# Hybrid decoder step on one core: the final norm's factors from a product with a matrix of ones, and the decode attention's output one step earlier in the output projection

## The chip, the core and the metric

The kernel runs on one core of a Trainium2 chip. A core has five engines that run side by side and wait for one another by semaphores: TensorE (PE; its weight loads are shown apart as PEld), VectorE (DVE), ScalarE (ACT), GpSimd (POOL) and SyncE (SP, which here only starts transfers). Each engine takes its instructions strictly in the order in which they were written into its queue. PE writes to the accumulator memory PSUM, which has eight banks; all else lies in the on-chip memory SBUF or in DRAM.

The metric is the device time of one execution in microseconds (us). The kernel before took a median of 1489.31 us in three runs (1488.1 to 1490.61).

## The reference

One layer of a decoder trunk over 1024 prompt tokens and 8 samples of one token each (T = 1032 columns in all). What the change touches:

```python
def rmsnorm(x, g):
    xf = x.astype(jnp.float32)
    y = xf * lax.rsqrt(jnp.mean(xf * xf, axis=-1, keepdims=True) + EPS)
    return (y * g.astype(jnp.float32)).astype(x.dtype)
...
oa_d = diff_attention(qa_d, k_all, v_all, pos_d, kpos_d, rel_bias, lam)
...
xd = xd + merge_groups(oa_d, o_rd, gr_d, subln_a[l], lam_init).astype(xd.dtype) @ w_out[l]
...
xp = xp + sq_relu_mlp(rmsnorm(xp, norm_mlp[l]), w_up[l], w_down[l])
...
y_prompt = rmsnorm(xp, norm_final)
y_sample = rmsnorm(xd, norm_final)
```

The output projection takes the attention's result for all 1032 tokens; the 8 samples' part needs each sample's attention over its cached values, normalized per head. The last step is a norm over the 1024 features of each token.

## The kernel before, in words

Everything is held transposed: features on the 128 partitions (eight groups `ft`), tokens along the row. A product in fp32 precision is made of three products of rounded halves (`UH`, `UL` for the operand, `wh`, `wl` for the weights), so each tile of the output projection has 8 x 3 = 24 matmuls. A scheduler places the instructions of a stage in the queues by its own estimate of the times; where `pin[0]` is set, PE keeps the order of the program. `issue_after` keeps an instruction from being placed ahead of another.

*The output projection* (`proj_residual`, tiles `pr_o`) runs over 8 feature groups and 3 column parts of 344 tokens, first parts 0 and 1 of all groups, then part 2, which holds the samples. The tile (ft, c) is added to the residual on DVE (line 1447), squared on ACT, and its squares are summed on GpSimd. Beside it runs a generator, `decode_values`, which makes the samples' attention output. After each tile listed in the argument `when` it takes one step: eight steps that gather a row of cached values and add its weighted sum to `dacc` on DVE; one that adds the new token's value; one (`dop`, `oda`) that sums `dacc` over groups of partitions on PE, copies the result, and normalizes it on DVE and GpSimd; and one (`dtr`) that transposes it on PE and splits it into `UH` and `UL`. Before the change, the last two steps were taken at the two places in `stage`: after tile (7, 1), the first half of part 2 for groups 0 and 1 is computed, then `dop`'s step is taken; then the first half for groups 2 to 4, then `dtr`'s. The second half of part 2 reads what `dtr` gave.

*The final norm* is made within the MLP's down projection (tiles `dn`), in its last group of steps, in program order. The steps n = 0 to 15 are the products for column half c = 0 (n = 0 to 7), then c = 1. The squares of the result are summed over the feature groups into `ssumf` (128 partitions by 1032 tokens). For each of the four quarters of tokens (c, half), 258 columns each, `finish_columns` and `finish_rows` run after the steps listed in two tables. `finish_columns` takes three pieces of 86 columns as stationary operands against a column of ones, so that the sums over partitions come out as 86 x 3; ACT takes the square root, DVE the reciprocal of that small tile (`factor_columns`). `finish_rows` spreads the factors back over 128 partitions by three products with the identity (`factor_rows`), and DVE multiplies the result's tiles by what stands in PSUM. For the second half the last tile's squares, `tails`, come as a second product and not through `ssumf`. The last quarter (1, 1) is finished after the last product of the program.

Of the kernel before, what the change touches and what calls it, by code (L numbers as in the profile page):

```python
# [10 lines left out]
F32 = mybir.dt.float32  # L11
# [8 lines left out]
P = 128  # L20
D = 1024
# [27 lines left out]
def decoder_step(ctx: ExitStack, tc: tile.TileContext, i: dict, o: dict):  # L49
    nc = tc.nc  # L50
# [1465 lines left out]
    with pool("x2") as XP:  # L1516
        x2 = [XP.tile([P, T], F32, tag=f"x2_{ft}", name=f"x2_{ft}") for ft in range(8)]
        g_mq = XP.tile([P, 8], F32, tag="g_mq", name="g_mq")
        nc.sync.dma_start(g_mq, i["g_mq"])
        with pool("c") as A:  # L1520
            def decode_values():
                def dt(name):
                    return PB.tile([P, 512], F32, tag="av", name=name, bufs=1)

                acc = A.tile([P, T], F32, tag="dacc", name="dacc")
                for k in range(8):
                    raw = A.tile([P, 1024], F32, tag="draw", name=f"cv_{k}", bufs=4)
                    gather(raw, i["cache_v"], idx, k)
                    with tc.issue_after(seen["DVE"]):
                        for x in range(8):  # L1530
                            c = slice(x * P, x * P + P)
                            w = at[:, x % 4, 2 * k + x // 4 : 2 * k + x // 4 + 1]
                            if k == 0:
                                nc.vector.tensor_scalar(acc[:, c], raw[:, c], w, None, ALU.mult)
                            else:
                                nc.vector.scalar_tensor_tensor(acc[:, c], raw[:, c], w, acc[:, c], ALU.mult, ALU.add)
# [8 lines left out]
                nc.vector.tensor_add(acc[:, :512], acc[:, :512], pd[:, :512])  # L1545
                yield

                with tc.issue_after(seen["PE"]):
                    op = dt("dop")
                    mm(op[:8, :], selgt, acc[:, 0:512], True, True)  # L1550
                    mm(op[32:40, :], selgt, acc[:, 512:1024], True, True)
                    od2 = A.tile([P, 1024], F32, tag="draw", name="oda", bufs=4)
                    oda, sqd = od2[:8, 0:512], od2[:8, 512:1024]
                    nc.scalar.copy(oda, op[32:40, :])
                    nc.vector.tensor_add(oda, oda, op[:8, :])
                    nc.vector.tensor_mul(sqd, oda, oda)
# [5 lines left out]
                    nc.vector.tensor_mul(odv, odv, r4.unsqueeze(2).to_broadcast([8, 4, P]))  # L1562
                yield
                with tc.issue_after(seen["PE"]):
                    tr = dt("dtr")
                    for h in range(4):
                        nc.tensor.transpose(tr[:, h * 8 : h * 8 + 8], oda[:, h * P : h * P + P], ident[:8, :8])
                    odT = tr[:, :32].rearrange("p (k c) -> p k c", k=4)
                    for h in range(4):
                        split_gain(odT[:, h, :], subln8, h, NT, T, gcol=0)  # L1570
                yield


            ssum = A.tile([P, T], F32, tag="ssum", name="ssum2")
            last = proj_residual(
                A, out_bank, U_OUT, OUT_KT, lambda ft: i["xT"][:, ft, :], lambda ft: x2[ft], ssum, "o", us_out, decode_values(),
                [(ft, c) for ft in range(4) for c in range(2)] + [(4, 1)],
                lambda x: [
                    G.tile([P, T], F32R, tag="rb2", name="wlo_3")[:, :1024] if (nm, x) == ("wl", 7)
                    else A.tile([P, 1024], F32R, tag=f"{nm}{x}", name=f"{nm}o_{x}") for nm in ("wh", "wl")  # L1580
                ],
                ahead=len(OUT_EARLY), early=early_out, stage=([(0, 2), (1, 2)], [(2, 2), (3, 2), (4, 2)]),
            )
# [392 lines left out]

    QP = QC // 3

    def factor_columns(bank, sums, last, x):
        col = bank[:QP, 300:303]  # L1980

        terms = [(y, j) for y in (sums, last) if y is not None for j in range(3)]
        for n, (y, j) in enumerate(terms):
            pinned(nc.tensor.matmul(
                col[:, j : j + 1], y[:, j * QP : j * QP + QP], ones[:, :1], start=n == 0, stop=n >= len(terms) - 3,
                skip_group_check=True))
        fc = KC.tile([QP, 3], F32, tag=f"fc{x % 2}", name=f"fc_{x}", bufs=2)
        nc.scalar.activation(fc, col, AF.Sqrt, scale=1.0 / D, bias=epsc[:QP])
        nc.vector.reciprocal(fc, fc)
        return fc  # L1990
# [7 lines left out]

    def norm_factor(x):
        fp = PD.tile([P, 512], F32, tag=("mk", "dt")[x % 2], name=f"rm_{x}", bufs=1)  # L2000
        FACTORS[x] = fp, factor_columns(fp, ssum[:, QCOLS[x]], None, x)

    def norm_rows(x):
        nc.scalar.copy(ssum[:, QCOLS[x]], factor_rows(*FACTORS[x]))
# [236 lines left out]
    with pool("acc", side="right") as AC, pool("rd", side="right") as RD, pool("w") as A, pool("w_ps", space=PSUM) as PS:  # L2241
# [19 lines left out]

        COLUMNS_AT, ROWS_AT, tails = {0: (0, 0), 3: (1, 0), 10: (0, 1), 15: (1, 1)}, {2: (0, 0), 5: (1, 0), 12: (0, 1), 15: (1, 1)}, {}
# [61 lines left out]
        ends = {}  # L2326

        def finish_columns(c, half):
            fp = PS.tile([P, 512], F32, tag=f"acc{turns[0] % 8}", name=f"fin_{c}_{half}", bufs=1)
            turns[0] += 1  # L2330
            ends[c, half] = fp, factor_columns(fp, ssf[:, QCOLS[2 * c + half]], tails[c] if half else None, 4 + 2 * c + half)
            for ft in range(8):
                y = C[((11, 21), (12, 22))[half][ft // 4]][:, ft % 4, c * QC : c * QC + QC]
                nc.scalar.activation(y, y, AF.Copy, scale=g_fin[:, ft : ft + 1])

        def finish_rows(c, half):
            cs = QCOLS[2 * c + half]
            rf = factor_rows(*ends[c, half])
            n = 2 if (c, half) == (1, 1) else 4
            for ft in range(0, 8, n):  # L2340
                y = C[((11, 21), (12, 22))[half][ft // 4]][:, ft % 4 : ft % 4 + n, c * QC : c * QC + QC]
                nc.vector.tensor_mul(y, y, rf.unsqueeze(1).to_broadcast([P, n, QC]))
                (nc.scalar if n == 2 and ft % 4 else nc.sync).dma_start(
                    o["yT"][ft * P : (ft + n) * P, cs].rearrange("(f p) c -> p f c", p=P), y)

        pin[0] = True
        for g in range(4):
# [26 lines left out]
            for new, qs, ps_ in parts:  # L2374
# [23 lines left out]
                for n, (q, p, c) in enumerate(steps):  # L2398
# [15 lines left out]
                    if g == 3:  # L2414
                        shared = C[0][:, p, cq]
                        for quad in {6: (21, 12), 7: (22,)}.get(q, ()):
                            nc.gpsimd.dma_start(C[quad][:, p, cq], shared, accum_op=ALU.add)
                        tail = None
                        if q in (2, 4, 5, 3):
                            tail = squares(INTO[q], p, c, (q, p) == (3, 3))  # L2420
                        if tail is not None:
                            tails[c] = tail
                        if end and n in COLUMNS_AT:
                            finish_columns(*COLUMNS_AT[n])
# [202 lines left out]
```

## Time and profile before

| | |
|---|---|
| Median of three runs | 1489.31 us (1488.1 to 1490.61) |
| The profiled execution | 1496.69 us, its span 1494.8 us |
| Busy share of PE, DVE, ACT, POOL | 98%, 73%, 45%, 21% |
| Output projection with decode output | about 455 to 537 us |
| Last products of the down projection | end at about 1484 us |
| From there to the end of the span | about 11 us |

A row of a timeline has the start in us, the duration in us, the engine, the line, the operation, what it writes and reads, the shape, the count, and in brackets the idle time ahead of it with what ended it. A piece of the chain has start, duration, engine, tile, line and count. A row of the windows has the stretch and its length, the busy time of PE, PEld, DVE, ACT and POOL with counts, the granted clock of TensorE, the share of the DMA engines, and GB/s. Matmuls overlap: a record is longer than the distance to the next. One fp32 matmul of the program shows as two records.

### The profile page before, as it was taken

How to read it: one execution, taken by the hardware profiler on the slowest of the kernel's cores; microseconds unless marked ns; L12 is line 12 of the kernel's file. 1: busy time of each engine (PE TensorE's matmuls, PEld its weight loads, DVE VectorE, ACT ScalarE, POOL GpSimd, SP SyncE). 2: the span in 40 equal slices, each digit the busy share in tenths (PEclk: the TensorE clock that was granted, in tenths of full speed). 3: DMA queues.
4: the chain of work that ended last, by engine and by line, in shares of the span. 5: the costliest groups of instructions: out<-in, count | busy, mean ns of one | idle time of the engine just before them, and what ended most of it. 6: DMA issues, size and time to landing. Idle time of an engine off the chain costs nothing.

```text
span 1494.8 us, 27880 instructions
## 1 busy us (share of the span) xinstructions
PE 1471.7 (98%) x10925; PEld 1401.8 (94%) x10925; DVE 1098.7 (73%) x2264; ACT 679.6 (45%) x1325; POOL 321.1 (21%) x346
## 2 busy tenths in 40 slices
PE   9999999998999999999999999999999999999997
PEld 7899779998779999989999999999999999999997
DVE  7666436887767636567886988888888879787865
ACT  7543435665552431248535643434334443343454
POOL 0035323123414311105022100000001311110380
PEclk9999999999999999999999999999999999999998
DMA  8255728213847157474582444344436774536273
GB/s 287 65 185 180 202 58 189 71 47 110 268 145 283 59 195 175 145 228 102 178 304 68 136 148 145 128 154 157 156 139 209 239 251 142 171 101 198 72 128 114
DMA packets 125238, 236.69 MB, mean 158 GB/s; under 512 B 13748, under 2 KB 76521, under 8 KB 124978
## 3 DMA queue, kind: packets, MB, share of 16 engines
q1 hardware_dynamic: 89064, 170.51, 36.0%
q0 software_dynamic: 24912, 44.80, 11.0%
q10 hardware_dynamic: 11130, 19.60, 3.5%
q8 instruction: 86, 1.41, 0.4%
q14 instruction: 46, 0.38, 0.1%
HBM read 170.25 MB, written 57.52 MB: 152 GB/s over the span
## 4 chain that ended last, share of the span: by engine, by line
PE 84%; DVE 8%; ACT 3%; issue 2%; DMA 2%; POOL 0%; ACTq 0%; another core or an unknown queue 0%; SPq 0%; DVEq 0%; POOLq 0%
PE dn L2309 19%; PE Z L2143 9%; PE qkp L75 7%; PE mq L75 6%; PE Y L2143 6%; PE X L2143 6%; PE pr_o L75 6%; PE pr_m L75 4%; PE grp L75 3%; PE sp L75 2%; PE av L75 2%; PE mv L75 1%; PE mk L75 1%; PE mpv L75 1%; PE vap_z L522 1%
## 5 line engine op out<-in xcount | busy, mean ns | idle before, releaser
L2309 PE MATMUL dn<-UH,wd 128*128 128x258 f32 x1792 | 325.1, 283 | 0.8 <-DVE c L2413 0.3
L2309 PEld LDWEIGHTS dn<-UH,wd 128*128 128x128 f32 x1792 | 277.6, 189 | 1.8 <-issue 0.8
L2309 PE MATMUL dn<-UL,wd 128*128 128x258 f32 x896 | 252.7, 282 | 0.0
L2309 PEld LDWEIGHTS dn<-UL,wd 128*128 128x128 f32 x896 | 169.0, 189 | 0.0
L2413 DVE TENSOR_TENSOR c<-c,dn 128x258 f32<-128x258 f32 x216 | 88.5, 417 | 38.2 <-PE dn L2309 35.8
L2169 ACT ACTIVATE hq<-r 128x258 f32<-128x258 f32 x128 | 53.9, 422 | 114.1 <-DVE r L2168 114.1
L2143 PE MATMUL X<-UH,wu 128*128 128x258 f32 x512 | 97.4, 282 | 0.9 <-ACT p L2194 0.9
L2143 PE MATMUL Z<-T_h,wu 128*128 128x258 f32 x512 | 98.2, 284 | 0.0
L2287 ACT CAST wd<-raw_d 128x512 fp32r<-128x512 f32 x96 | 58.8, 620 | 78.4 <-PE dn L2309 73.2
L1953 ACT CAST wu<-raw_up 128x512 fp32r<-128x512 f32 x96 | 59.2, 617 | 62.2 <-PE Z L2143 54.7
L2280 ACT CAST UH<-raw_h 128x1032 fp32r<-128x1032 f32 x56 | 58.8, 1057 | 55.0 <-PE dn L2309 27.3
L2143 PEld LDWEIGHTS X<-UH,wu 128*128 128x128 f32 x512 | 81.3, 188 | 1.1 <-ACT p L2194 1.1
L2143 PEld LDWEIGHTS Z<-T_h,wu 128*128 128x128 f32 x512 | 81.3, 189 | 0.0
L2281 DVE TENSOR_TENSOR UL<-raw_h,UH 128x1032 fp32r<-128x1032 f32 x56 | 73.4, 1311 | 9.9 <-ACT UH L2280 9.9
L2180 POOL DMA_DIRECT2D HT<-ht x32 | 17.2, 536 | 292.4 <-DVE ht L2179 291.9
L2288 DVE TENSOR_TENSOR wd<-raw_d,wd 128x512 fp32r<-128x512 f32 x96 | 72.0, 757 | 10.0 <-ACT wd L2287 9.9
L2143 PE MATMUL Z<-T_l,wu 128*128 128x258 f32 x256 | 72.3, 282 | 0.0
L2143 PE MATMUL X<-UL,wu 128*128 128x258 f32 x256 | 72.3, 282 | 0.0
L128 ACT CAST wh_u<-raw_u 128x1024 fp32r<-128x1024 f32 x43 | 44.7, 1049 | 54.2 <-PE mq L75 31.2
L1954 DVE TENSOR_TENSOR wu<-raw_up,wu 128x512 fp32r<-128x512 f32 x96 | 64.5, 684 | 3.7 <-ACT wu L1953 3.7
L129 DVE TENSOR_TENSOR wl_u<-raw_u,wh_u 128x1024 fp32r<-128x1024 f32 x39 | 51.6, 1328 | 18.3 <-ACT wh_u L128 18.1
L2301 POOL TENSOR_TENSOR raw_d<-raw_d,raw_d 128x512 f32<-128x512 f32 x16 | 22.1, 1382 | 194.5 <-DVE raw_d L2297 173.4
(598 smaller groups left out, 4718.2 us busy)
## 6 DMA issues: line engine op xcount, KB each, us to landing
raw_u<-in_wall SPq DMA_DIRECT2D x49, 512.0 KB
HT<-ht POOLq DMA_DIRECT2D x32, 516.0 KB
raw_h<-HT SPq DMA_DIRECT2D x32, 516.0 KB
raw_up<-in_wall SPq DMA_DIRECT2D x32, 512.0 KB
raw_d<-in_wall SPq DMA_DIRECT2D x32, 512.0 KB
HQ<-hq ACTq DMA_DIRECT2D x32, 387.0 KB
raw_h<-HQ SPq DMA_DIRECT2D x24, 516.0 KB
cmk<-in_cmk SPq DMA_DIRECT2D x16, 512.0 KB
```

Of the source, the lines that this page charges most:

```text
L75: pinned(nc.tensor.matmul(out, l, r, start=start, stop=stop))
L129: (lo_engine or nc.vector).tensor_sub(wl[:, :n], raw[:, :n], wh[:, :n].bitcast(F32))
L1953: nc.scalar.copy(w[:, :512], src)
L1954: nc.vector.tensor_sub(w[:, 512:], src, w[:, :512].bitcast(F32))
L2143: pinned(nc.tensor.matmul(ps, l, r[:, k, :], start=first and k == 0 and x == 0, stop=k == 3 and x == 2, skip_group_check=True))
L2169: nc.scalar.activation(h[:, PLACE[quad], :], r, AF.Square)
L2280: nc.scalar.copy(h, rv)
L2281: nc.vector.tensor_sub(l, rv, h.bitcast(F32))
L2287: nc.scalar.copy(w[:, :512], src)
L2288: nc.vector.tensor_sub(w[:, 512:], src, w[:, :512].bitcast(F32))
L2309: pinned(nc.tensor.matmul(ps, l, r[:, k, cq], start=first and k == 0 and x == 0, stop=k == 3 and x == 2, skip_group_check=True))
L2413: nc.vector.tensor_add(y, y, ps)
```

## The change

```diff
@@ decode_values, proj_residual's arguments
                     for h in range(4):
                         split_gain(odT[:, h, :], subln8, h, NT, T, gcol=0)
                 yield
+                yield
...
-                [(ft, c) for ft in range(4) for c in range(2)] + [(4, 1)],
+                [(ft, c) for ft in range(4) for c in range(2)] + [(4, 1), (5, 1)],
@@ final norm
-        def finish_columns(c, half):
-            fp = PS.tile([P, 512], F32, tag=f"acc{turns[0] % 8}", name=f"fin_{c}_{half}", bufs=1)
-            turns[0] += 1
-            ends[c, half] = fp, factor_columns(fp, ssf[:, QCOLS[2 * c + half]], tails[c] if half else None, 4 + 2 * c + half)
+        def finish_sums(c, half):
+            f = acc_bank(f"fin_{c}_{half}")
+            y = ssf[:, QCOLS[2 * c + half]]
+            mm(f, onesq, y, True, not half)
+            if half:
+                mm(f, onesq, tails[c], False, True)
+            nc.scalar.activation(f, f, AF.Sqrt, scale=1.0 / D, bias=epsc)
+            nc.vector.reciprocal(y, f)
             for ft in range(8):
...
         def finish_rows(c, half):
             cs = QCOLS[2 * c + half]
-            rf = factor_rows(*ends[c, half])
+            rf = ssf[:, cs]
```

*The decode output.* The list `when` has one more entry, so the step with `dop` is taken after tile (5, 1); `dtr`'s moves to the first place in `stage`, and the added `yield` leaves the second place empty.

*The final norm.* One product of a 128 x 128 matrix of ones (`onesq`, which the kernel already held) with the 258 columns of sums gives the sum over partitions on all 128 partitions at once. The root is taken in PSUM and the reciprocal written back over `ssumf`, both 128 x 258 and no longer 86 x 3, and the scaling reads SBUF. The three small products, the three products with the identity, and the second half's three small ones fall away; the second half has two products with the ones. `factor_columns` and `factor_rows` stay for the norm ahead of the MLP; their argument `last` goes, since only the final norm used it. Its instructions there are the same.

What the scheduler made of the first part, on PE in the projection. The names are the tile that is written and what is read; `pr_o_0_...` with `who_5057` is the second half of the weights of tile (6, 0), `pr_o_2_...` are tiles of part 2. Before, around `dop`:

```order
L75 MATMUL pr_o_2_5388<-UH,wh_u_4611 128x344
L75 MATMUL pr_o_2_5388<-UL,wh_u_4611 128x344
L75 MATMUL pr_o_2_5388<-UH,wl_u_4612 128x344
L75 MATMUL dop<-dacc,selgt 8x512 x2
L75 MATMUL pr_o_2_5414<-UH,wh_u_4698 128x344
L75 MATMUL pr_o_2_5414<-UL,wh_u_4698 128x344
```

and with the change:

```order
L75 MATMUL pr_o_0_5272<-UL,who_5057 128x344
L75 MATMUL pr_o_0_5272<-UH,wlo_5058 128x344
L75 MATMUL pr_o_0_5272<-UH,who_5057 128x344
L75 MATMUL dop<-dacc,selgt 8x512 x2
L75 MATMUL pr_o_0_5272<-UL,who_5057 128x344
L75 MATMUL pr_o_0_5272<-UH,wlo_5058 128x344
```

`dop` now stands within tile (6, 0), behind 16 of its 24 matmuls; `dtr` stands where `dop` stood, behind the first half of the second tile of part 2.

On DVE in the same stretch, as a difference (`x_6`, `x_7`: the residual's tiles, written by line 1447):

```order
 L1545 TENSOR_TENSOR dacc<-dacc,pdv_5198 128x512
 L1447 TENSOR_TENSOR x_5_4942<-pr_o_1_5230,x_5_4942 128x344
-L1447 TENSOR_TENSOR x_6_4943<-pr_o_0_5259,x_6_4943 128x344
-L1447 TENSOR_TENSOR x_6_4943<-pr_o_1_5288,x_6_4943 128x344
-L1447 TENSOR_TENSOR x_7_4944<-pr_o_0_5317,x_7_4944 128x344
+L1555 TENSOR_TENSOR oda<-oda,dop 8x512
+L1447 TENSOR_TENSOR x_6_4943<-pr_o_0_5272,x_6_4943 128x344
+L1556 TENSOR_TENSOR oda<-oda 8x512
+L1558 TENSOR_REDUCE ds_5266<-oda 8x4
+L139 TENSOR_SCALAR ds_5266<-ds_5266 8x4
+L1562 TENSOR_TENSOR oda<-oda,dr_5268 8x512
+L1447 TENSOR_TENSOR x_6_4943<-pr_o_1_5301,x_6_4943 128x344
```

The five instructions on `oda` stood behind all eight UL splits of parts 0 and 1; now they stand right behind the sum `dacc`, among the additions of tiles (6, 0) and (6, 1).

On DVE at the end of the program, before:

```order
L2324 TENSOR_TENSOR ssumf<-ssumf,sqc_f_1_1_17288 128x258
L2324 TENSOR_TENSOR ssumf<-ssumf,sqc_f_2_1_17304 128x258
L2413 TENSOR_TENSOR c_13388<-c_13388,dn_5_3_1_17235 128x258
L1989 RECIPROCAL fc_17329<-fc_17329 86x3
L2342 TENSOR_TENSOR c_13388<-c_13388,fin_1_17322 128x2x258 x2
```

and with the change:

```order
L2323 TENSOR_TENSOR ssumf<-ssumf,sqc_f_1_1_17268 128x258
L2414 TENSOR_TENSOR c_13388<-c_13388,dn_5_3_1_17218 128x258
L2323 TENSOR_TENSOR ssumf<-ssumf,sqc_f_2_1_17284 128x258
L2332 RECIPROCAL ssumf<-fin_1_17302 128x258
L2343 TENSOR_TENSOR c_13388<-c_13388,ssumf 128x2x258 x2
```

The last addition of squares into `ssumf` moved behind the addition of the last product, and the reciprocal is 128 x 258. On the other engines the order outside these two places is the same as before.

More of the change, by code (lines that the diff above doesn't have):

```diff
@@ L1977, in decoder_step, with factor_columns @@
     QP = QC // 3
-    def factor_columns(bank, sums, last, x):
+    def factor_columns(bank, sums, x):
         col = bank[:QP, 300:303]
-        terms = [(y, j) for y in (sums, last) if y is not None for j in range(3)]
-        for n, (y, j) in enumerate(terms):
+        for j in range(3):
             pinned(nc.tensor.matmul(
-                col[:, j : j + 1], y[:, j * QP : j * QP + QP], ones[:, :1], start=n == 0, stop=n >= len(terms) - 3,
-                skip_group_check=True))
+                col[:, j : j + 1], sums[:, j * QP : j * QP + QP], ones[:, :1], start=j == 0, stop=True, skip_group_check=True))
         fc = KC.tile([QP, 3], F32, tag=f"fc{x % 2}", name=f"fc_{x}", bufs=2)
@@ L2000, in norm_factor @@
         fp = PD.tile([P, 512], F32, tag=("mk", "dt")[x % 2], name=f"rm_{x}", bufs=1)
-        FACTORS[x] = fp, factor_columns(fp, ssum[:, QCOLS[x]], None, x)
+        FACTORS[x] = fp, factor_columns(fp, ssum[:, QCOLS[x]], x)
     def norm_rows(x):
@@ L2260, in residual_rows @@
                 nc.sync.dma_start(C[quad][:, x], X3[kh + x.start : kh + x.stop, :, hs].rearrange("k p c -> p k c"))
-        COLUMNS_AT, ROWS_AT, tails = {0: (0, 0), 3: (1, 0), 10: (0, 1), 15: (1, 1)}, {2: (0, 0), 5: (1, 0), 12: (0, 1), 15: (1, 1)}, {}
+        SUMS_AT, ROWS_AT, tails = {0: (0, 0), 3: (1, 0), 10: (0, 1), 15: (1, 1)}, {2: (0, 0), 5: (1, 0), 12: (0, 1), 15: (1, 1)}, {}
         INTO = {1: 0, 2: 11, 6: 0, 7: 22, 4: 21, 5: 22, 3: 12}
@@ L2324, in squares @@
             (nc.vector if quad in (22, 12) else nc.gpsimd).tensor_add(ssf[:, cs], ssf[:, cs], sq)
-        ends = {}
-        def finish_columns(c, half):
-            fp = PS.tile([P, 512], F32, tag=f"acc{turns[0] % 8}", name=f"fin_{c}_{half}", bufs=1)
-            turns[0] += 1
-            ends[c, half] = fp, factor_columns(fp, ssf[:, QCOLS[2 * c + half]], tails[c] if half else None, 4 + 2 * c + half)
+        def finish_sums(c, half):
[6 more added lines that the diff above has]
+            nc.vector.reciprocal(y, f)
             for ft in range(8):
@@ L2422, in decoder_step @@
                             tails[c] = tail
-                        if end and n in COLUMNS_AT:
-                            finish_columns(*COLUMNS_AT[n])
+                        if end and n in SUMS_AT:
+                            finish_sums(*SUMS_AT[n])
                         if end and n in ROWS_AT:
```

## The prediction

> **What bounds the kernel now.** I read the page first, then the waits of TensorE (PE), then the two places that the diff touches, as timelines, windows and pieces of the chain.
>
> ```profile
> span 1494.8 us, 27880 instructions
> PE 1471.7 (98%) x10925; PEld 1401.8 (94%) x10925; DVE 1098.7 (73%) x2264; ACT 679.6 (45%) x1325; POOL 321.1 (21%) x346
> PE 84%; DVE 8%; ACT 3%; issue 2%; DMA 2%; POOL 0%; ACTq 0%; another core or an unknown queue 0%; SPq 0%; DVEq 0%; POOLq 0%
> PE dtr L1567 <- DVE oda L1562: 1.0, 1, 1.0
> ```
>
> PE holds 84% of the chain that ended last. So a microsecond taken from PE's stream, or added to it, is a microsecond of the end; work on VectorE (DVE), ScalarE (ACT) or GpSimd (POOL) counts only where PE waits for it, or after PE's last product. Of the waits, one belongs to a place in the diff: the transposes `dtr` wait 1.0 us for `oda`. The other place is the end of the program.
>
> **Part 1: the decode output moves up.** Before the change:
>
> ```profile
> 479.37 26.64 PE pr_o L75 x168
> 480.00:490.00 10.00, 10.00 (x66) 10.00 (x65) 10.00 (x30) 1.71 (x4) 5.33 (x3) 1.00 0.19 61
> 491.05 0.77 DVE L1545 TENSOR_TENSOR dacc<-dacc,pdv 128x512 f32<-128x512 f32 x1
> 491.74 0.93 DVE L1447 TENSOR_TENSOR x<-pr_o,x 128x344 f32<-128x344 f32 x2
> 494.70 0.52 DVE L1447 TENSOR_TENSOR x<-pr_o,x 128x344 f32<-128x344 f32 x1 [2.02 <-PE pr_o L75]
> 505.93 1.03 PE L75 MATMUL dop<-dacc,selgt 128*8 128x512 f32 x4
> 506.89 0.43 PE L75 MATMUL pr_o<-UH,wh_u 128*128 128x344 f32 x1
> 513.82 0.38 PE L1567 MATMUL dtr<-ident,oda 8*128 8x8 f32 x4 [1.00 <-DVE oda L1562]
> ```
>
> *Removed:* with `dop` some 100 matmuls earlier, `oda` is ready long before the transposes, and their wait of 1.00 us goes.
>
> *Added:* a wait of `dop`, which reads `dacc`. That sum ends at 491.05 + 0.77 = 491.82, because DVE has no pause before it (10.00 busy in 480 to 490) and runs behind PE. When does PE now come to `dop`? The row at 494.70 waited for PE, so it marks the end of tile (6,1), 494.66. A matmul of this stream takes 26.64 / 168 = 0.159 us, a tile of 24 takes 3.8, so tile (6,0) ended at 490.87. In the new order `dop` stands behind 16 of its 24 matmuls: 8 x 0.159 = 1.27 before that end, and 0.16 of drain earlier (a record lasts 0.32, the next starts after 0.16): 489.44. PE takes its work in order, so everything behind `dop` waits until 491.82: **2.4 us of new stall**. In the old place `dop` came 14.1 us after its operand and waited for nothing. Its own cost, 505.93 to 506.89, is the same in both places.
>
> *Who else waits:* on DVE the chain of `oda` now stands ahead of the additions of tiles (6,1) and (7,0), with GpSimd's power in its middle.
>
> ```profile
> 507.00 0.58 ACT L1554 COPY oda<-dop 8x512 f32<-8x512 f32 x1
> 510.26 0.68 DVE L1556 TENSOR_TENSOR oda<-oda 8x512 f32<-8x512 f32 x1
> 511.92 1.04 POOL L140 TENSOR_TENSOR dr<-ds,half 8x4 f32<-8x4 f32 x1 [5.84 <-DVE ds L139]
> 512.99 0.68 DVE L1562 TENSOR_TENSOR oda<-oda,dr 8x512 f32<-8x512 f32 x1 [1.15 <-POOL dr L140]
> 513.60 1.21 DVE L129 TENSOR_TENSOR wl_u<-raw_u,wh_u 128x1024 fp32r<-128x1024 f32 x1
> 516.41 0.23 DVE L145 SCALAR_TENSOR_TENSOR UL<-dtr,subln,UH 128x8 fp32r<-128x8 f32 x1 [0.34 <-ACT UH L144]
> ```
>
> From 491.87: `dop` 1.03, copy 0.58, four wide DVE passes at about 0.68 with one tile addition (0.5), small ones and the power 1.04 between: about 498. Tile (6,1) itself then ends at 494.66 + 2.4 + 0.96 = 498.0, so its addition is not late. The transposes, now at 505.93 + 2.4 + 0.96 = 509.3, are split on ACT and DVE as before (513.82 to 516.64, 2.8 us), with one weight split (1.21) in between: 513.3. PE first runs 36 matmuls (5.7 us) and needs them from 515.3 on. I cost that at nothing; if DVE's earlier splits, which shift with PE, eat these 2 us, it is a few tenths.
>
> Part 1: 2.4 - 1.0 = **+1.4 us**. Bounds: -1.0 if DVE is in time for `dop`; above, one for one with DVE's lateness (a rival below).
>
> **Part 2: the end, inside PE's stream.** Three of the four factor groups stand between the products. Their pieces in the chain, and a product of the same kind as the new one (fp32, 128x128 stationary, 512 columns):
>
> ```profile
> 1458.44 0.39 PE fin L1984 x6
> 1461.81 0.64 PE fin L75 x6
> 1463.93 0.39 PE fin L1984 x6
> 1467.29 0.63 PE fin L75 x6
> 1475.16 0.85 PE fin L1984 x12
> 1478.99 0.65 PE fin L75 x6
> 457.72 0.86 PE rp L75 x2
> 1455.00:1484.00 29.00, 28.98 (x251) 28.77 (x249) 19.92 (x40) 16.56 (x40) 2.45 (x3) 1.00 0.31 99
> ```
>
> Removed: 0.39 + 0.64 + 0.39 + 0.63 + 0.85 + 0.65 = 3.55 us. Added: four products of 258 columns, 0.86 x 258 / 512 = 0.43 each, 1.73. **-1.8 us.** Bounds: -1.0 if each cost the 0.64 that three pieces of 86 columns cost together, and -2.0 at 0.39. The square root becomes 258 wide on ACT and the reciprocal 258 wide on DVE; neither is waited for here, since the products go on in other banks. DVE's additional passes (about 1.1 each) fit beside: over the 29 us of the last row it is busy for 19.92.
>
> **Part 3: behind the last product.** PE's last product ends at 1483.70 + 0.28 = 1483.98, the scaling starts at 1487.78: 3.80 us.
>
> ```profile
> 1483.70 0.28 PE L2309 MATMUL dn<-UH,wd 128*128 128x258 f32 x1
> 1484.06 0.42 DVE L2413 TENSOR_TENSOR c<-c,dn 128x258 f32<-128x258 f32 x1
> 1484.51 0.42 ACT L2317 ACTIVATE sqt<-c 128x258 f32<-128x258 f32 x1 [0.22 <-DVE c L2413]
> 1484.99 0.63 PE fin L1984 x6
> 1485.64 0.27 ACT fc L1988
> 1485.94 0.18 DVE fc L1989
> 1486.16 1.60 PE fin L75 x6
> 1487.78 0.69 DVE c L2342
> L1013 DVE RECIPROCAL mn<-sm x32: 151/158/164, 256.4 to 422.7; 128x1 f32<-128x1 f32 x32
> L1067 DVE RECIPROCAL c<-sm x4: 184/187/196, 283.5 to 419.6; 128x8 f32<-128x8 f32 x4
> 1484.00:1486.00 2.00, 1.24 (x12) 1.07 (x12) 0.54 (x3) 1.48 (x4) 0.00 (x0) 1.00 0.60 164
> 1486.00:1487.80 1.80, 1.58 (x6) 1.36 (x6) 0.12 (x2) 0.00 (x0) 0.00 (x0) 0.51 0.03 10
> ```
>
> The product with the identity, 1.60 us at a granted clock of 0.51, falls away. What comes, from the last product's end: the last addition ends at +0.50 as now; one addition of squares is now ordered behind it and ends at +0.84 (0.34 each, back to back); two products of 0.43 and the drain, +1.91; the wide root at the 0.42 of the squares (same engine and width), +2.35. The reciprocal has no wide row. Eight columns take 187 ns, one takes 158: 4.1 ns a column, so 258 take 158 + 257 x 4.14 = **1.22 us**, and the scaling starts at +3.65. Gain **0.15 us**. Bounds: at the rate of the 258-wide addition (0.42 us) 0.95 is gained; at the steepest reading of the two rows, (196 - 151) / 7 = 6.4 ns a column, 1.80 us, 0.43 is lost. I take 1.22, since the two medians are the nearest rows, though far from 258. The products come before 1486, where the clock was still 1.00.
>
> The Trainium skill, "VectorE: DVE Perf Modes", section "First, the fixed hardware budget", says that the reciprocal runs as an iterative divide with a repeat count of 8; were that eight cycles a column at the page's 0.96 GHz, an estimate from the page, 258 columns would take about 2.3 us and the sum would end 1.1 us later. The two rows show half that slope.
>
> **Sum.** +1.4 - 1.8 - 0.15 = -0.6 us. The profiled execution took 1496.69 us (span 1494.8); it would take 1496.1. The median of the runs, 1489.31, is 7.4 lower; the terms are the same in it: **1488.7 us**. A measurement of this kernel can tell about 0.2%, 3.0 us, from no change.
>
> **Rivals.**
> *A: DVE is in time and `dop` doesn't stall.* For it: the timed runs are 7.4 us shorter than the profiled one, so something runs more smoothly there; and of DVE's groups of eight weighted sums ahead of `dacc` some took 2.17, others more:
>
> ```profile
> 483.61 3.13 DVE L1536 SCALAR_TENSOR_TENSOR dacc<-cv,at,dacc 128x128 f32<-128x128 f32 x8
> 487.08 2.18 DVE L1536 SCALAR_TENSOR_TENSOR dacc<-cv,at,dacc 128x128 f32<-128x128 f32 x8
> ```
>
> Against it: 2.4 us must be found, and DVE is full for 20 us before. Time: -1.0 - 1.8 - 0.15 = -3.0, 1486.3; with the reciprocal at its fast bound 1485.5.
> *B, the other side: slower, since `dop` waits longer than the trace lets one see.* The place is PE at `dop`; each microsecond by which `dacc` ends later is one of the end, where before 14.1 us of cover lay between. It outweighs the gains from a stall of 1.0 + 1.8 + 0.15 = 3.0 us, `dacc` at 492.4, 0.6 later than traced. With 3 us more it gives +2.4: 1491.7. For it: one slow group of sums (3.13 for 2.18) costs 1 us. Against: the timed runs are shorter than the traced one.
> *C: the wide reciprocal is as dear as its upper bound.* The tail loses 0.43 in place of gaining 0.15: 1489.3. The page named in part 3 points this way.
>
> **Chances.** Forecast 0.60 (own range 1487.5 to 1490.1: the upper end adds the bounds of parts 2 and 3, +1.4 - 1.0 + 0.43), A 0.17, B 0.11, C 0.12. Range: from A with the fast reciprocal, 1485.5, to most of B, 1491.0. Faster by over 0.2% (below 1486.3): half of A and a little of the rest, 0.13. Slower by over 0.2% (above 1492.3): half of B, 0.06. Within: 0.81.
>
> **What would show it.** In the changed kernel's trace: a wait of `dop` for `dacc` of about 2.4 us near 489.4 and none of `dtr`; `fin` products at 0.43 us each; the wide reciprocal near 1.2 us; the scaling 3.65 us behind the last product. I am wrong if `dop` shows no wait, or if the new `dtr` splits hold up PE, or if the reciprocal is far from 1.2.

## The result, and the profile after

The changed kernel took 1489.89 us (median of 22 runs, 1487.88 to 1493.14) against 1488.07 us of the kernel before in the same rounds (22 runs): a ratio of 1.0015 with a 95% interval of 1.0009 to 1.0021, slower by 2.2 us (1.3 to 3.1). A second measurement (e12) gave 1.0015 again (1.0006 to 1.0024). The forecast was 0.6 us faster: the change lies within 0.2% as forecast, but on the other side.

The profiled execution of the changed kernel took 1488.14 us. From its page the span, the busy times and the chain's shares by engine; and from TensorE's waits the rows at the two places of the change (us in total, times, the longest of them):

```profile
span 1486.3 us, 27786 instructions
PE 1464.9 (99%) x10877; PEld 1395.6 (94%) x10877; DVE 1101.5 (74%) x2264; ACT 677.3 (46%) x1325; POOL 320.9 (22%) x346
PE 83%; DVE 8%; issue 3%; DMA 2%; ACT 2%; POOL 1%; ACTq 0%; DVEq 0%; POOLq 0%
```

```profile
PE dop L75 <- DVE dacc L1545: 2.3, 1, 2.3
PE fin L75 <- DVE ssumf L2323: 0.9, 1, 0.9
```

The wait of `dtr` is gone, and `dop` waits 2.3 us in its place. The span is 8.5 us shorter than that of the profiled execution before, while the runs are slower. Most of that (5.5 us) is the stretch from the first `sp` to the first `pr_o`, 177.7 us here and 183.2 before, which the change doesn't touch. A total of two profiles says nothing here; stages have to be compared, and over several profiles.

The products of the new norm in TensorE's stream, as pieces of the chain (start, duration, engine, tile, line, count):

```profile
1451.86 0.44 PE fin L75 x2
1456.62 0.43 PE fin L75 x2
1467.15 0.87 PE fin L75 x4
```

They cost 1.74 us where the prediction had 1.73. The tail, as a timeline (start, duration, engine, line, operation, count, idle time before it), and the group of the wide reciprocals:

```profile
1474.94 0.28 PE L2308 MATMUL dn<-UH,wd 128*128 128x258 f32 x1
1475.60 0.42 DVE L2323 TENSOR_TENSOR ssumf<-ssumf,sqc_f 128x258 f32<-128x258 f32 x1
1476.07 0.70 PE L75 MATMUL fin<-ssumf,onesq 128*128 128x258 f32 x2 [0.85 <-DVE ssumf L2323]
1476.61 0.60 PE L75 MATMUL fin<-sqt,onesq 128*128 128x258 f32 x2
1477.25 0.45 ACT L2331 ACTIVATE fin<-fin,epsc 128x258 f32<-128x258 f32 x1 [0.57 <-PE fin L75]
1477.73 1.77 DVE L2332 RECIPROCAL ssumf<-fin 128x258 f32<-128x258 f32 x1 [1.71 <-ACT fin L2331]
1479.53 1.91 DVE L2343 TENSOR_TENSOR c<-c,ssumf 128x516 f32<-128x516 f32 x3
```

```profile
L2332 DVE RECIPROCAL ssumf<-fin x4: 1760/1770/1771, 1452.8 to 1477.7; 128x258 f32<-128x258 f32 x4
```

From the last product's end (1475.22) to the scaling it is 4.31 us, not 3.65. Up to the root the steps came as worked out (products end at +1.99, forecast +1.91). The reciprocal took 1.77 us, close to the upper bound of 1.80 and not to the 1.22 that was chosen.

Against the before profile's 3.80 us that is half a microsecond more. With the other terms (+1.1 at `dop` in this profile, -2.1 in the product stream) the two profiles give -0.5 us, and the runs say +2.2. The experiments look for the rest.

### The profile page after: what moved, and what is told of

It is laid out like the page before. It is cut to its first block, busy times and chain, and to the rows that moved or that the text cites. A ratio compares the mean times of both kernels' runs of the same rounds, so it can differ in the third digit from the quotient of the medians.

```text
span 1486.3 us, 27786 instructions
## 1 busy us (share of the span) xinstructions
PE 1464.9 (99%) x10877; PEld 1395.6 (94%) x10877; DVE 1101.5 (74%) x2264; ACT 677.3 (46%) x1325; POOL 320.9 (22%) x346
## 4 chain that ended last, share of the span: by engine, by line
PE 83%; DVE 8%; issue 3%; DMA 2%; ACT 2%; POOL 1%; ACTq 0%; DVEq 0%; POOLq 0%
PE dn L2308 19%; PE Z L2142 9%; PE qkp L75 7%; PE mq L75 6%; PE Y L2142 6%; PE X L2142 6%; PE pr_m L75 4%; PE grp L75 3%; PE pr_o L75 3%; PE sp L75 2%; PE av L75 2%; PE mv L75 2%; PE mk L75 1%; PE mpv L75 1%; PE vap_z L522 1%
```

## The experiments

Names used in the expectations: T, the terms that the traces show are all there is; N, the norm's part loses more than the traces show; P, the projection's part loses more, since a later stage passes its delay on; and, from the second set on, G, the pause at `dop` also makes TensorE's clock fall. All runs with a ratio were timed beside the kernel before on the same chip; 0.001 is 1.5 us.

**e1, the projection's part alone.** The kernel before with (`...` marks lines left out of an edit)

```diff
                 yield
+                yield
...
-                [(ft, c) for ft in range(4) for c in range(2)] + [(4, 1)],
+                [(ft, c) for ft in range(4) for c in range(2)] + [(4, 1), (5, 1)],
```

> The projection's part alone, on the kernel before. Theory T (what the two traces show at the changed places): dop waits 2.3 us for dacc, dtr no longer waits 1.0; +1.3 us, and the stretch from vrep to the last rs product longer by about 1.1 us. Rival N (the norm's part is what loses): also +1.3 or less here. Rival P (the projection loses more than the place itself shows, by a shift that another stage passes on or enlarges): +2.5 us or more, with the additional time in a stage behind the projection.

Ratio 1.0026 (1.0015 to 1.0036), +3.9 us (2.2 to 5.4): more than T's 1.3, and as much as P had it.

**e2, the norm's part alone.** The changed kernel with the two lines above undone.

> The final norm's part alone, on the kernel before. Theory T: PE's stream -1.8 us, +0.5 by waits of the products for DVE, which is full with 1.77 us reciprocals, and +0.3 to +0.5 behind the last product: about -1 us. Rival N: +0.5 us or more, with the loss in DVE's backlog of the last 30 us. Rival P: -1 to -2 us.

Ratio 0.9990 (0.9977 to 1.0002), -1.5 us. The loss is the projection's; N falls. The +0.5 us of waits in the expectation was misread: those waits stand elsewhere (part 2 below).

**e3, the projection's step one tile pair later.** As e1 with (6, 1) in the place of (5, 1).

> The projection's part alone, but with the decode output's step after tile (6,1) and not after (5,1), so that dop stands behind 24+24 matmuls of tiles (6,0) and (6,1), some 5 us later. Theory T: no wait of dop and none of dtr, -1.0 us against the kernel before and 2.3 less than with the step after (5,1). Rivals N and P: as T at this place, but P leaves the loss of a later stage where it is, so 0 to +1.5.

Ratio 0.9982 (0.9973 to 0.9991), -2.7 us (-4.0 to -1.3), with no wait of `dop` or `dtr`; that is faster than any of the three had it. e1 and e3 differ by one number in a list and by 6.6 us in the ratios' centres (4.6 in the medians); the pause in e1 is 2.35 us. What comes behind that pause shows in e1's timeline and its windows (stretch and length, PE busy and its count, granted clock, DMA share, GB/s):

```profile
490.27 1.03 PE L75 MATMUL dop<-dacc,selgt 128*8 128x512 f32 x4 [2.35 <-DVE dacc L1545]
491.66 0.49 PE L75 MATMUL pr_o<-UH,who 128*128 128x344 f32 x1
495.08 0.32 PE L75 MATMUL pr_o<-UH,who 128*128 128x344 f32 x1
```

```profile
490.00:491.00 1.00, 0.73 (x4) 1.00 0.00 0
491.00:492.00 1.00, 1.00 (x6) 0.81 0.00 0
492.00:493.00 1.00, 1.00 (x5) 0.50 0.00 0
493.00:494.00 1.00, 1.00 (x6) 0.50 0.00 0
494.00:495.00 1.00, 1.00 (x5) 0.50 0.00 0
495.00:496.00 1.00, 1.00 (x8) 0.98 0.00 0
```

The clock falls to 0.50 for 3.41 us (491.62 to 495.04, from windows of half a microsecond); a record lasts 0.49 us in place of 0.32. PE is "busy" all the while, so neither the busy share nor the waits show it. Half of 3.41 us is 1.7 us, on top of the pause. In e3 the clock stays at 1.00. The stretch from `vrep` to `rs`, which holds the place, is 59.8 us in e1, 55.7 in e3, 57.0 before: 4.1 us between e1 and e3.

**e4, the reciprocal made cheap.** e2 with

```diff
-            nc.vector.reciprocal(y, f)
+            nc.vector.tensor_copy(y, f)
```

> The final norm's part alone with the four 128x258 reciprocals replaced by copies of the same size (so the result is scaled by the root and not by its inverse). A copy from PSUM should take about 0.42 us and not 1.77. Theory T: the wait of the products for DVE goes (-0.5) and the tail is 1.35 shorter, so 1.8 us less than with the reciprocals, about -2.8 against the kernel before. Rival N: even more than that comes back, 2.5 us or more. Rival P: 1.35 us less than with the reciprocals.

This kernel leaves out the inverse, so its results are scaled by the root. Ratio 0.9975 (0.9966 to 0.9984), 2.2 us below e2 (2.9 in the medians). The copy that stands in for the reciprocal:

```profile
L2331 DVE COPY ssumf<-fin x4: 426/426/426, 1458.0 to 1482.6; 128x258 f32<-128x258 f32 x4
```

1.34 us less each. `dn` runs from first to last product in 325.6 us (e2: 325.4), so the three reciprocals inside the stream cost nothing. The fourth is on the path: the tail is 1.8 us shorter (last product's start to the end of the span, 9.6 and 11.4 us).

**e5, the pause filled.** The projection's part with the step behind (6, 0) and, ahead of that tile's own products,

```diff
+                if (ft, c) == (6, 0):
+                    for _ in range(14):
+                        mm(ps[:, :CH], units[0][0][0][:, :P], UH[:, 4, :CH], True, True)
```

> The projection's part alone, but TensorE is kept busy where it waited: 14 products of 128x344 whose result is overwritten stand ahead of (6, 0)'s own, and the decode output's step comes after (6, 0), so that its product is issued some 2.2 us (14 x 0.159 us) + 1.3 us later than in e1 and finds dacc done (estimate 492.9 against 491.8). TensorE is late by the same 2.2 to 2.3 us as in e1, but by work and not by a pause. Theory G (the pause of e1 makes the granted clock fall to half for about 3.4 us, some 1.7 us on top of the pause, in part of the executions): no fall of the clock after dop, stretch vrep to rs 58.2 us (57.0 - 1.0 + 2.2), total +1.2 us against before, some 1.7 us less than e1. Theory T (only the pause counts, the low clock in e1's profile is chance): the same +1.2 us. Theory P (whatever delays the projection by 2 us costs 3 to 4 in all, because a later stage passes the shift on): +3 to +4 us as e1, at a clock that stays up.

Ratio 0.9990 (0.9978 to 1.0002). `dop` doesn't wait, the clock stays at 1.00, the stretch is 58.0 us. P falls: PE comes out of the place 2.3 us later than in e3, and nothing is lost beyond that. The kernel came out 2.7 us better than forecast, outside its interval (the forecast +1.2 is 1.0008). Part of it is given back later: the first products of the up projection wait 1.6 us for ScalarE in e3, and not at all here. Why is not shown: that they come later is no reason, since in e1, where they come later still, they wait 1.6 us too.

**e8, half the pause.** The projection's part with the step behind (6, 0), nothing filled in.

> The projection's part alone with the decode output's step after (6, 0): its product is issued 1.3 us later than in e1 (8 more products of 0.159 us ahead of it), so the wait for dacc is 1.1 us and not 2.3. dtr's 1.0 us is gone as in e1. Theory T (the pause alone): +0.1 us against before. Theory G: +0.1 us if a pause of 1.1 us with the two decode products (1.0 us) behind it is too short to make the clock fall, +1.8 us if it still does; the rows of the clock around 490 to 495 us say which. Theory P: more than +0.1 at a clock that stays up.

Ratio 0.9995 (0.9981 to 1.0009).

```profile
488.67 1.03 PE L75 MATMUL dop<-dacc,selgt 128*8 128x512 f32 x4 [0.92 <-DVE dacc L1545]
```

The clock doesn't fall, and the stretch is 56.8 us, 1.1 more than e3's: a pause of 0.9 us costs about its length.

**e6, the last quarter left in the old way.** The kernel before with the norm's part alone, but `finish_columns` and `finish_rows` do (1, 1) as before the change:

```diff
+            if (c, half) == (1, 1):
+                ...
+                ends[c, half] = fp, factor_columns(fp, ssf[:, QCOLS[2 * c + half]], tails[c] if half else None, 4 + 2 * c + half)
+            else:
                 f = acc_bank(f"fin_{c}_{half}")
...
-            rf = ssf[:, cs]
+            rf = factor_rows(*ends[c, half]) if (c, half) == (1, 1) else ssf[:, cs]
```

> The norm's part alone, but the last of the four quarters keeps the old way through columns and rows; the three quarters inside the product stream use the matrix of ones and the wide reciprocal. Traces' sum: three quarters of the gain in TensorE's stream (3 x 4 chain products saved between the quarters, e2 read about -2 in dn's first to last product) and nothing in the tail: last product to end as before (3.8 us from the last product to the scaling, not 4.3). Expected -1.5 to -2 us against before, about 0.5 us less than e2. If the reciprocal's 1.77 us in VectorE's stream costs more than the traces show (theory N), e6 is like e2 (-1.1 to -1.5) or above.

Ratio 0.9980 (0.9967 to 0.9994), -3.0 us. That is 1.5 us below e2 by the ratios, but the intervals overlap; this run alone doesn't tell them apart.

**e7, e6 and e3 together.** No pause, three quarters new, the last one old.

> The norm as in e6 together with the decode output's step after (6, 1) as in e3: no wait for dtr, none for dacc, no chain products in three quarters, the old tail. Sum of the measured parts: e3 (-1.7 to -2.7) and e6 (expected -1.5 to -2): -3 to -4.7 us against before. By the traces' sum alone (T): -1.0 - 1.7 = -2.7. If the two parts get in each other's way, less than either sum.

Ratio 0.9965 (0.9952 to 0.9978), 1488.43 against 1493.06 us: 5.2 us (3.3 to 7.2) faster than the kernel before, where the change as made loses 2.2. The sum of the measured parts (-3 to -4.7) was nearer than that of the traces (-2.7), which lies outside the interval.

**e9, pauses measured by themselves.** Behind the last product, dense blocks, and between them pauses made by chains of copies on VectorE (kind 1, 3, 5, 7, 10 copies; D, five copies and two 8-column products; S, no pause but 16 products with 8 columns):

```diff
+        ps, first, count = dense("gap_start", 80), None, 0
+        for rep in range(6):
+            for kind in (1, 3, 5, 7, 10, "S", "D"):
...
+                count += 1
+                ps = dense(f"den{kind}_{rep}", 74 + 5 * (count % 6), first)
```

> The kernel before with a test stretch behind its last product (its time is not compared): 42 dense blocks of 74 to 99 products of 128x258, and between them, six times each, a pause in which TensorE waits for a chain of 1, 3, 5, 7 or 10 copies of 128x258 on VectorE; or no pause but 16 products whose moving operand has 8 columns, as opm's; or the pause of five copies with two products of an 8-column stationary behind it, as at dop. Theory G as the ten profiles so far have it (falls of the clock begin at points that are a fixed 3.413 us grid within one execution, and cost 1.71 us each): after every pause the clock either stays at 1.00 or falls to 0.50 for 3.41 us, beginning on one grid through the whole stretch; the shortest pauses (estimate below 1 us) never make it fall, pauses near dop's 2.3 us do in part of the six, depending on where they lie on the grid, the longest (estimate above 3.4 us) always; opm-like products in part of the six, since the same stage lost 1.7 us in 4 profiles of 10. Rival R1 (a fixed delay after the pause, no grid): the falls begin at one distance behind each pause's start and a given length of pause always or never makes the clock fall. Rival R2 (the low clock at dop was chance or the place's own): hardly any fall here.

Three of the pauses in the timeline (the idle time in brackets), and the granted clock in the 5 us around each:

```profile
1516.65 0.50 PE L2434 MATMUL den<-pt,wd 128*128 128x258 f32 x1 [1.84 <-DVE pt L2440]
1531.60 0.39 PE L2434 MATMUL den<-pt,wd 128*128 128x258 f32 x1 [2.50 <-DVE pt L2440]
1708.05 0.39 PE L2434 MATMUL den<-pt,wd 128*128 128x258 f32 x1 [1.84 <-DVE pt L2440]
```

```profile
1516.00:1521.00 5.00, 4.35 (x23) 0.66 0.00 0
1529.00:1534.00 5.00, 2.50 (x21) 1.00 0.00 0
1706.00:1711.00 5.00, 3.16 (x26) 1.00 0.00 0
```

A pause of 1.84 us made the clock fall, one of 2.50 didn't, and another of 1.84 didn't either. So it isn't the length alone. The falls, from windows of a quarter of a microsecond, begin at 1482.63 (in the kernel's own tail) and then 21 times in the test stretch, the last at 2059.49. The distance between first and last is 169 x 3.4134 us, and all 22 beginnings have the same remainder in units of 3.4133, to 0.01 us. Each fall lasts 3.41 us or twice that (four times: behind two of the longest pauses and two of the runs of small products). So time is cut into a fixed grid of cells of 3.413 us, and at a cell's end it is decided whether the clock is halved in the next one. With the grid known, each pause can be cut by it. The first one above, 1514.81 to 1516.65, lay whole in the cell that ended at 1516.77. The second, 1529.10 to 1531.60, was cut at 1530.42 into 1.32 and 1.18 us.

| Between the blocks | falls of 6 | most idle time in one cell, with a fall | without |
|---|---|---|---|
| pause of 0.52 us | 0 | | 0.52 |
| pause of 1.18 us | 0 | | 1.18 |
| pause of 1.84 us | 4 | 1.84 | 1.58, 1.70 |
| pause of 2.50 to 2.59 us | 2 | 2.36, 2.59 | 1.32 to 1.70 |
| pause of 3.58 us | 6 | 2.21 to 3.31 | |
| pause of 1.84 us, two 8-column products | 4 | 1.81 to 1.84 | 0.94, 1.35 |
| no pause, 16 products with 8 columns (3.5 us) | 5 | 2.42 to 3.24 of small products | 1.99 |

The line lies between 1.70 and 1.81 us of idle time in one cell, about half a cell. R1 falls (the pauses of one length behave differently), and so does R2. The last row of the table shows that PE needn't be idle: the small products count as busy in every view and still make the clock fall.

The Trainium skill, "TensorE: Matmul & The Clock Gate", section "What's actually happening", says that the clock is set by a free-running window of 4096 cycles, 3413 ns, at half or full rate; the 22 beginnings agree to 0.01 us. The same page's section "Why this matters for your kernels" advises no idle gaps above about 3 us. This stretch sets the line lower: 1.84 us is enough where it lies within one cell.

**e10, the changed kernel with the step behind (6, 1).**

> The changed kernel with the decode output's step one bank later than in the change, after (6, 1). Theory G and T: neither dop nor dtr waits, TensorE has no pause there; e2 + e3 measured apart gives -1.1 to -1.5 and -1.7 to -2.7, so -2.8 to -4.2 us against before, and 4 to 6 us less than the changed kernel in this job (pause 2.3 + the clock's up to 1.7 + noise of about 1). Rival P: the projection's move itself loses, wherever the step stands: no better than before by more than 1.5.

Ratio 0.9978 (0.9969 to 0.9987), -3.3 us. The whole change is a gain once `dop` doesn't wait.

**e11, the changed kernel with the pause filled as in e5.**

> The changed kernel with the pause at dop filled: 14 overwritten products of 128x344 (2.2 us) stand ahead of (6, 0)'s own, and the step comes after (6, 0). TensorE is as late as with the pause, but never idle. Theory G: the changed kernel's time less the clock's fall, at most 1.7 us less, so +0.1 to +1.8 against before by the traces' sum; 2.2 us more than the changed kernel with the step after (6, 1). Theory T: the same as the changed kernel. What would speak against both: as fast as the step after (6, 1), so that 2.2 us of products cost nothing there.

Ratio 0.9981 (0.9972 to 0.9991). What was to speak against both came: it is as fast as e10, within 2 us. By the traces it should be 1.3 us behind e10 (the place 58.0 against 55.7 us, and the up projection's wait for ScalarE 0 against 1.0), which the intervals can't exclude. Against the changed kernel (e12), filling the same time with overwritten products gains 5.1 us (about 3 to 7). So it is the pause that costs, and not the delay. Its price is only in part accounted for: over the six profiles of the changed kernel the place is 1.2 us longer than here (59.15 against 58.0, 59.8 in the four where the clock falls), and the up projection waits 0.7 us on average against nothing. The rest, some 3 us, shows in no stage of these profiles, so it is not shown that the halved clock is all that a pause costs on top of its length.

**e12, the changed kernel beside them.**

> The changed kernel itself, on the same chip as the three others and in the same rounds, as their point of comparison; and a second profile of the place at dop. +1.8 us against before (as measured before: 1.0009 to 1.0021), the pause of 2.3 us at dop in the profile, with or without the clock's fall behind it.

Ratio 1.0015 (1.0006 to 1.0024). Its profiled execution was the shortest of its twelve, 1491.12 us against a median of 1495.21, and the clock didn't fall behind `dop` in it. So four more profiles of it follow.

**e13 to e16, the changed kernel four more times.**

> The changed kernel, one more profile. The test stretch with pauses had the clock fall where at least 1.81 us of idle time lay inside one cell of the 3.413 us grid, and not at 1.70 or less; by that the clock falls behind dop's pause of 2.3 us in about half of the executions, stretch vrep to rs then 59.5 us (58.1 + 1.7 less what overlaps), otherwise 57.7 to 58.1. If the pause itself is longer in a typical execution, dop's wait is above 3 us. If it is neither, the stretch vrep to rs is 58 us and the time sits in another stage.

> As the look before it: the clock's fall behind dop in about half of the looks, by where the pause lies in the grid's cell; dop's wait 1.9 to 2.4 us.

> As the look before it: the clock's fall behind dop in about half of the looks, by where the pause lies in the grid's cell; dop's wait 1.9 to 2.4 us.

> As the look before it: the clock's fall behind dop in about half of the looks, by where the pause lies in the grid's cell; dop's wait 1.9 to 2.4 us.

They took 1495.62, 1494.51, 1494.34 and 1491.29 us, and the clock fell behind `dop` in all four. `dop` in e16, then in e12, then in e13, and the clock behind it in e14:

```profile
489.65 1.03 PE L75 MATMUL dop<-dacc,selgt 128*8 128x512 f32 x4 [1.92 <-DVE dacc L1545]
```

```profile
489.73 1.03 PE L75 MATMUL dop<-dacc,selgt 128*8 128x512 f32 x4 [1.88 <-DVE dacc L1545]
```

```profile
491.84 1.88 PE L75 MATMUL dop<-dacc,selgt 128*8 128x512 f32 x4 [2.61 <-DVE dacc L1545]
```

```profile
491.00:492.00 1.00, 0.99 (x5) 1.00 0.00 0
492.00:493.00 1.00, 1.00 (x6) 0.52 0.00 0
493.00:494.00 1.00, 1.00 (x5) 0.50 0.00 0
494.00:495.00 1.00, 1.00 (x6) 0.50 0.00 0
495.00:496.00 1.00, 1.00 (x7) 0.77 0.00 0
```

In e13 and e15 the fall caught `dop` itself (1.88 us for 1.03). The grid of each execution can be read from its other falls, so the pause can be cut by it in all seven profiles that hold it:

| | wait of `dop` | of it in one cell | clock | `vrep` to `rs` |
|---|---|---|---|---|
| after | 2.33 | 1.51 | stays | 58.1 |
| e12 | 1.88 | 1.88 | stays | 57.7 |
| e16 | 1.92 | 1.92 | falls | 59.2 |
| e1 | 2.35 | 2.06 | falls | 59.8 |
| e14 | 2.32 | 2.32 | falls | 59.7 |
| e13 | 2.61 | 2.54 | falls | 59.9 |
| e15 | 2.94 | 2.93 | falls | 60.3 |

The line at this place lies between 1.88 and 1.92 us, a little above that of the test stretch; why is not shown. The first profile of the changed kernel had drawn a position that cuts the pause in two.

## Why the prediction was wrong

**Part 1: right in its mechanism, and its size is what failed.** `dtr`'s wait went, `dop`'s came, at 1.9 to 2.9 us where 2.4 was worked out; nothing else at the place waited, and `oda` was ready long before the transposes. The step that fails is "2.4 us of new stall", which took a pause of PE to cost its length. In six profiles of the changed kernel (the first, and e12 to e16) the place takes 59.15 us on average against 57.0 in all five profiles with the old projection (e9's counted): **+2.15 us, not +1.4**. Where the clock stays up it is +1.1 and +0.7, a little less than forecast; where it falls, in four of six, +2.2 to +3.3. Most of that difference is the halved clock's 1.7 us, which e1 and e9 show by themselves, as e5 and e8 show its absence. Rival A falls, `dop` waits in every profile. Rival B had the place right and the mechanism only in part: in no profile did the wait pass its break-even of 3.0 us by its length (the longest is 2.94), but with the clock's fall the price did. P, that a delay of this size costs more in a later stage, falls with e5 and e11, where as long a delay by work does not.

**Part 2: right.** -1.8 us was forecast; from `dn`'s first to last product five profiles with the old norm (e9's left aside) take 327.2 us on average (326.3 to 328.1), ten with the new one 325.1 (324.0 to 326.2): **-2.1**. That VectorE's passes fit beside was right too. VectorE is full for a stretch, but TensorE doesn't wait there (a row of the windows of the changed kernel):

```profile
1455.00:1465.00 10.00, 10.00 (x84) 9.94 (x83) 10.00 (x18) 5.15 (x13) 0.00 (x0) 1.00 0.49 167
```

The page has 0.8 us in which `dn` waits for VectorE, and the expectations of e2 and e4 took them for a cost of the wide reciprocals. The timeline puts them some 250 us ahead of the new norm, in stages that the change leaves alone:

```profile
1194.35 0.39 PE L2308 MATMUL dn<-UH,wd 128*128 128x258 f32 x1 [0.38 <-DVE c L2414]
1202.20 0.36 PE L2308 MATMUL dn<-UH,wd 128*128 128x258 f32 x1 [0.39 <-DVE c L2414]
```

**Part 3: two steps failed.** First, "the reciprocal has no wide row ... 1.22 us". It took 1.77, +0.55. The two medians from 1 and 8 columns gave 4.1 ns a column; from one column (158 ns) to 258 it is 6.3 ns. The steepest reading of the same two rows, 6.4, came close, by luck: it sets the slowest of one row against the fastest of the other. Rival C had the mechanism of this half. The Trainium skill, "VectorE: DVE Perf Modes", section "First, the fixed hardware budget", with its repeat count of 8, gave an estimate of 2.3 us, too high by as much as mine was too low.

Second, the "3.80 us" from the last product to the scaling, against which the new tail was held. It contains the product with the identity at 1.60 us, with the clock at 0.51. The argument took the low clock for a property of the tail. It was that execution's place on the grid (its fall began at 1486.02). In e3, whose tail is the old one, the timeline reads

```profile
1478.26 0.28 PE L2310 MATMUL dn<-UH,wd 128*128 128x258 f32 x1
1480.72 0.90 PE L75 MATMUL fin<-ident,fc 86*128 86x86 f32 x6 [0.56 <-DVE fc L1990]
1481.66 1.90 DVE L2343 TENSOR_TENSOR c<-c,fin 128x516 f32<-128x516 f32 x3 [0.99 <-PE fin L75]
```

0.90 us at full clock, and 3.12 us in all. It is 0.91 as a piece of the chain in e1, e3, e5 and e8 alike, and 0.90 in e9. In e6 and e7, which finish the last quarter in the old way, it is 1.58 and 1.11: there the fall came early in the tail again. So the old tail is 3.1 us where the fall comes later, in five profiles of eight, the new one 4.3, and the change loses **1.2 us** there where 0.15 of gain was forecast (about 1.0 with the early falls averaged in). This is the largest error of the sum. The span agrees: from the last product's start to its end it is 10.0 to 10.1 us in e1, e3, e5 and e8, 11.2 to 11.4 in the nine profiles of the new tail.

**The sum** with the measured sizes is +2.15 - 2.1 + 1.2 = +1.25 us, against 2.2 (1.3 to 3.1) in the runs, and -0.6 forecast. About 1 us is not found, at the edge of what the measurement tells, and two things that the sum leaves out pull it either way. The two profiles without the fall behind `dop` were the second fastest of 22 runs and the fastest of 12, so an ordinary execution is likelier to be like the other four, with +2.8 us at the place (this is argued, not shown). And the stretch from `opm` to the first `X`, which the change doesn't touch, took 45.0 us in all five profiles with the old projection, but 43.5 in four of the six of the changed kernel: 1.0 us less on average. The last section comes back to it. The runs, split by parts, add up: the projection +3.9 (2.2 to 5.4), the norm -1.5 (-3.4 to +0.3), together +2.4. The projection's 3.9 is more than its 2.15 in the traces. The norm's part is a gain in the stream that the last quarter gives back by half; the projection's part would be a gain of 1.3 us of place (55.7 against 57.0) if it were one tile pair later.

That the forecast time, 1488.7 us, lies only 1.2 below the measured 1489.89 is luck: the kernel before took 1488.07 in these rounds and not the 1489.31 that the forecast started from. The change itself was missed by 2.8 us.

Of the marks that were set: the wait of `dop`, the missing wait of `dtr` and the 0.43 us products came as said; "the reciprocal is far from 1.2" is what came true of the list of ways to be wrong. That the clock could fall in the middle of the program was not on it, though it stood in the profile before. There the clock falls twice ahead of the tail, at 356.21 and 786.29 us, each for 3.41 us; read in windows of 100 us it shows only as 0.98.

## What to carry to other kernels

A wait of TensorE is not priced by its length alone: ask whether about 1.8 us of it can fall into one 3.4 us cell of the clock's grid, and add 1.7 us times the chance of that, as a lower bound (filling the pause gained 5 us in e11); below it (0.9 us in e8) the wait cost only itself. When an operand may be late, move its consumer back until it is surely ready, since a place too early cost 5 us here and two tiles later cost nothing that showed (e12 and e10). And before a stage's length from a single profile is used as the baseline, look at the granted clock within it. A rate worked out from rows far from the new shape is a range and not a number: here 1 and 8 columns gave 4.1 ns a column by their medians and 6.4 at the steepest, and 258 columns came out at 6.3.

## What the runs showed of the hardware

The clock's grid does not move within an execution (the falls of one profile agree on it to 0.02 us) and differs from one to the next (its offset from the span's start lies between 0.1 and 3.2 us of 3.41), so identical instructions cost differently in different executions. The stretch from `opm` to the first `X`, with the same rows in the same order, is 45.0 us (44.9 to 45.0) in 7 of 17 profiles (all but e9's) and 43.4 to 43.5 in the other 10; the difference is one fall of the clock behind `opm`'s 8-column products. With e9's, that fall stands in all five profiles with the old projection and in 3 of the 13 with the moved one. If the eight falls were spread by chance over the 18 profiles, those five would all have one in under 1 case of 100. So a stage moved in one place may decide whether the clock falls 300 us later; no run here tests it. Another fall stands between 349 and 359 us in 14 of the 17. These falls, a microsecond and a half each, would account for part of the several microseconds over which runs of one kernel spread.

A reciprocal of 128x258 fp32 takes 1.77 us on VectorE and a copy of that shape 0.43; one column takes 158 ns and eight 187. The wide one cost nothing among the products and all of itself behind the last one (e4).
